# A hybrid decoder step on one core: where the attention's loads and stores stand in the DMA queue

## The chip, the cores and the metric

The kernel runs on one core of a Trainium2 chip. The metric is device time of the whole program in microseconds; the time before is the median of three runs. A profile of one further execution gives the trace that all rows below come from. Engines are PE (matrix multiplication, PEld its weight loads), DVE, ACT, POOL, and SP, which here does nothing but issue DMAs, one after another, in the order of its program. An SP instruction that waits for a buffer holds everything behind it.

## The reference

One inference step of a decoder with one recurrent layer (RG-LRU) and one attention layer with forget gates (FoX), for a prompt of 2048 new tokens and for 8 sequences of 8 new tokens with 4096 cached tokens each. Keys, values and log forget values are made once after the recurrent layer. The attention and what follows it, cut to what matters:

```python
def fox_block(q, k, v, cq, ck, q_pos, k_pos):
    s = jnp.einsum('bqhd,bkhd->bhqk', q, k).astype(jnp.float32) * (HEAD_DIM ** -0.5)
    s = s + jnp.swapaxes(cq, 1, 2)[:, :, :, None] - jnp.swapaxes(ck, 1, 2)[:, :, None, :]
    mask = k_pos[None, :] <= q_pos[:, None]
    s = jnp.where(mask[None, None], s, -jnp.inf)
    p = jax.nn.softmax(s, axis=-1)
    return jnp.einsum('bhqk,bkhd->bqhd', p.astype(v.dtype), v)
...
def fox_mixer(x, k, v, cq, ck, q_pos, k_pos, w_in, w_out):
    z = x @ w_in
    q, g = z[..., :D_ATTN].reshape(B, T, N_HEADS, HEAD_DIM), z[..., D_ATTN:]
    o = fox_attention(q, k, v, cq, ck, q_pos, k_pos).reshape(B, T, D_ATTN)
    return (o * jax.nn.silu(g)) @ w_out
...
past_k = cache_k[page_table].reshape(Bs, past_len, N_HEADS, HEAD_DIM)
past_v = cache_v[page_table].reshape(Bs, past_len, N_HEADS, HEAD_DIM)
```

There are 16 heads of 64, and a page of the cache holds 128 tokens. For the prompt, keys are the new tokens themselves; for the 8 sequences they are 32 cached pages each and the 8 new tokens. Everything is float32.

## The kernel before

The program runs in phases: the recurrent layer, the projections to keys, values, queries and gates (phase_b), the attention of the prompt, and the output projection. The decode, which is the attention of the 8 sequences over their cached pages, has no phase of its own: it is a generator (decode, line 1038) that a Side object (line 1011) advances a little after every step of the projections or of the prompt's attention. So two streams of work are interleaved on all engines.

**The order of instructions.** The Python code traces instructions one after another. A scheduler of the framework then puts the instructions of each engine into their final order, by a modelled timeline, with the order of tracing as priority: an instruction whose inputs and buffer are modelled as free earlier can be placed ahead of one that was traced before it. On the chip the order is fixed, and each instruction waits for semaphores where it stands. Two helpers add order by hand: issue_after(ins) places what a block traces on the engine of ins behind ins, without any wait for ins to finish; behind("V" or "T", ins) does the same against the newest instruction that the dictionary `place` holds for DVE or PE.

**The decode.** A turn is one sequence and half of its heads; there are 16, two of them in an early decode and 14 in the one that runs beside the later projections and the attention (called with ahead=True, lines 1812 to 1820). A turn reads 8 groups of 4 key pages and 8 groups of 4 value pages. pages (line 1075) issues one group, here called a page for short: four DMAs of 256 KB (line 1088) into one of 4 buffers named raw. DVE transposes a key page into ktr (line 1173), PE multiplies it with the queries into dS (line 1141); PE multiplies a value page with the numerators sx into dO (line 1251). Between keys and values stands softmax (line 1181): maxima, exponentials, sums, then a DVE transpose into sy, which takes a raw buffer for it, four stores of sy to DRAM (pd, line 1231), and a load back in another layout (sx, line 1232). period (line 1287) interleaves value pages 5 to 7 of the previous turn and key pages of the next one with steps of softmax: after each of the first seven pages two steps of it are taken, in the order v5, k0, v6, k1, v7, k2, k3, and what is left of it before v0.

**The prompt's attention** (line 1323) goes through 16 heads; a head has four units, one for each chunk of 512 queries, in rising order in even heads (4, 8, 12 and 16 blocks of 128 keys) and falling in odd ones. One block of scores is one step of the loop at line 1551, a tick: 40 ticks a head, 640 in all. A tick has two matmuls of scores (lines 1557 and 1558: qa with ka, qbt with kbt), an exponential on ACT into p or, for the first block, acc (line 1566), and every four ticks the products with the values vvt into ops (line 1577), after which POOL adds p into acc. Row maxima for units ahead are made by advance (line 1512) through the matmuls sx of line 1420 and DVE reductions (lines 1422 and 1424).

The loads of attention, all on SP but the very first:

- load_low(u + 2) at the start of unit u loads qa, 256 KB, 4 buffers (line 1408);
- load_keys (lines 1388 and 1389) loads kbt of the next head at tick 0 of a head;
- load_head (lines 1395 and 1396) loads ka (1 MB, 2 buffers) and vvt (512 KB) of the next head at tick 3;
- load_unit (line 1402) loads qbt as advance needs it.

After every second head norm (line 1481) inverts the sums and for each of the four chunks fetches the gates sgt (line 1501, 2 buffers), multiplies them with the head pair's output on POOL and with the inverted sums on DVE, and stores the product to og_d (line 1497). A Later object (line 349) runs closures a given number of ticks on: fetches at 3, 5, 7 and 9 ticks, each gate 3 ticks after its fetch, its store with it. For the last head pair the chunks go one by one as they end. The output projection reads og_d.

Of the kernel before, what the change touches and what calls it, by code (L numbers as in the profile page):

```python
# [20 lines left out]
P = 128  # L21
# [6 lines left out]
H = 16  # L28
# [29 lines left out]
ADD = "G"  # L58
OG = 1
NQ = 6  # L60


class Turns:
# [23 lines left out]
def tile_hawk_fox(  # L87
# [8 lines left out]
    V, A, G, T, S = nc.vector, nc.scalar, nc.gpsimd, nc.tensor, nc.sync  # L96
# [12 lines left out]
    place = {}  # L109

    def behind(engine, ins):

        if engine in place:
            tc.add_manual_dep(ins, place[engine].name, ORDER)

    def together(mms, after=(), beside=False):

# [53 lines left out]
    og_d = [dt_(f"ogd{qc}", [D, 512]) for qc in range(SEQ // 512)]  # L171
# [866 lines left out]
    def decode(es, turns, nraw, nktr, ahead):  # L1038
# [36 lines left out]
        def pages(cache, b, hg, g):  # L1075

            with ExitStack() as order:

                if len(last) >= 3:
                    order.enter_context(tc.issue_after(last[-3]))  # L1080
                regs = nc.values_load_multi_w_load_instructions(
                    pt1[0:1, b * NPG + g * 4:b * NPG + g * 4 + 4], engines=[SP], min_val=0, max_val=NPOOL - 1,
                    skip_runtime_bounds_check_because="the table was held between the first page and the last")[1]
            raw = pool.tile([P, 4, 512], F32, name="raw", tag="raw", bufs=nraw)
            came = []
            for i in range(4):
                page = cache[ds(regs[i], 1), :, hg * 8:(hg + 1) * 8, :]
                d = S.dma_start(raw[:, i, :], page.rearrange("o k h d -> (o k) (h d)"))
                came.append(d)
            last.append(d.ins)  # L1090
            return raw, came

        def new_rows(rows, b, hg):
# [87 lines left out]
        def softmax(t):  # L1181

            dl = t.dl
            b, hg, gmx = t.b, t.hg, t.gmx
            if not ahead:
                t.raws = [pages(cache_v, b, hg, x) for x in range(2)]
            while dl.q:
                dl.tick()
                yield HOP

            V.tensor_reduce(mx[:, :8], gmx[:, :, :].rearrange("p g h -> p h g"), axis=AX.X, op=ALU.max)
            mp = bank("dm")
            T.transpose(mp[:, :P], mx[:, :], ident[:, :])
            m1 = pool.tile([8, DS], F32, name="dm1", tag="dm1")
            V.tensor_reduce(m1[:, :], mp[:8, :P].rearrange("h (a q) -> h q a", q=DS), axis=AX.X, op=ALU.max)
            V.tensor_scalar(mr[:8, :, :], m1[:, :].unsqueeze(1).to_broadcast([8, 16, DS]), -1.0, 0.0, op0=ALU.mult, op1=ALU.add)
            T.matmul(mp[:, P:P + 8], mr[:, :, :].rearrange("h a q -> h (a q)"), ident[:, :8], start=True, stop=True)
            nm = pool.tile([P, 8], F32, name="dnm", tag="dnm")
            V.tensor_copy(nm[:, :], mp[:, P:P + 8])
            if t.next and t.next[1] == 0:  # L1200
                fetch_q(t.next[0])
            yield 3 * HOP

            ss = pool.tile([P, 2, 8], F32, name="dss", tag="dss")
            tt(V, t.cn[:, :, :], t.cn[:, :, :], nm[:DS, :].unsqueeze(2).to_broadcast([DS, 8, DS]), ALU.add)
            A.activation(pn[:DS, :, :DS], t.cn[:, :, :], AF.Exp)
            V.tensor_reduce(ss[:DS, 1, :], pn[:DS, :, :DS], axis=AX.X, op=ALU.add)
            for j in range(4):
                for h in (2 * j, 2 * j + 1):
                    A.activation(t.sc[:, :, h, :], t.sc[:, :, h, :], AF.Exp, bias=nm[:, h:h + 1], accum_out=ss[:, 0, h:h + 1])  # L1210
                if t.next:
                    place_q(*t.next, j)
                yield HOP
            tt(V, ss[:DS, 0, :], ss[:DS, 0, :], ss[:DS, 1, :], ALU.add)
            dg = pool.tile([P, 8, DS], F32, name="ddg", tag="ddg")
            tt(V, dg[:, :, :], ss[:, 0, :].unsqueeze(2).to_broadcast([P, 8, DS]),
               qmask[:, :].unsqueeze(1).to_broadcast([P, 8, DS]), ALU.mult)
            sp = bank("dsum")
            T.matmul(sp[:, :64], ones[:, :], dg[:, :, :].rearrange("p h q -> p (h q)"), start=True, stop=True)
            rb = t.rb = pool.tile([P, 64], F32, name="drb", tag="drb", bufs=2)  # L1220
            V.reciprocal(rb[:, :], sp[:, :64])


            sy = spare()[:, :].rearrange("p (a x h q) -> p a x h q", a=4, x=8, h=8)
            for h in range(8):
                V.transpose(sy[:, :, :, h, :].rearrange("p a x q -> p x a q"), t.sc[:, :, h, :])

            sx = pool.tile([P, 4, 8, 8, DS], F32, name="sx", tag="sx")
            pd = pd_d[(b * 2 + hg) % 2]
            for i in range(4):  # L1230
                S.dma_start(pd[:, :, i].rearrange("a l f -> l a f"), sy[i * 32:(i + 1) * 32].rearrange("p a x h q -> p a (x h q)"))
            S.dma_start(sx[:, :, :, :, :].rearrange("p i x h q -> p (i x h q)"), pd.rearrange("a l i f -> (a l) (i f)"))
            pt = pool.tile([32, 8, 32], F32, name="dpt", tag="dpt")
            V.transpose(pt[:, :, :].rearrange("p h x -> p (h x)"), pn[:, :, :].rearrange("p h x -> p (h x)"))
            pc = t.pc = pcs[(b * 2 + hg) % 2]
            A.copy(pc[:32, :].rearrange("p (h q) -> p h q", h=8), pt[:, :, :DS])
            t.sx = sx
# [85 lines left out]
    def attention(es):  # L1323
# [67 lines left out]
        def load_head(h):  # L1391
            hr = slice(h * HD, (h + 1) * HD)
            ka = pool.tile([P, SEQ], F32R, name="ka", tag="ka", bufs=2)
            for lo, hi in halves(h):
                queue[0].dma_start(f(ka[:, lo:hi]), kd_d[h * HD:(h + 1) * HD, :, lo:hi].rearrange("d x t -> (d x) t"))
            queue[0].dma_start(vvs[h % 2][:, :, :], v_d[:, hr].rearrange("(k p) d -> p k d", p=P))
            heads[h] = ka
# [6 lines left out]
        def load_low(u):  # L1404
            if u < len(units):
                h, qc = units[u]
                qa = qas[u] = pool.tile([P, 512], F32R, name="qa", tag="qa", bufs=4)
                queue[0].dma_start(f(qa[:, :]), qd_d[h * HD:(h + 1) * HD, :, qc * 512:(qc + 1) * 512].rearrange("d x t -> (d x) t"))
# [72 lines left out]
        def norm(pr, sums, q0, n, oT):  # L1481

            ps_ = slice(q0 * 32, (q0 + n) * 32)
            V.reciprocal(sums[ps_, :], sums[ps_, :])
            rs = [pool.tile([P, 32], F32R, name=f"rs{x}", tag=f"rs{x}") for x in range(2)]
            V.tensor_copy(rs[0][ps_, :], sums[ps_, :])
            tt(V, rs[1][ps_, :], sums[ps_, :], f(rs[0][ps_, :]), ALU.subtract)
            for x in range(2):
                to = rr[x * 8:(x + 1) * 8, :] if n == 4 else rr[x * 8 + q0:x * 8 + q0 + 5:4, :]
                S.dma_start(f(to).rearrange("j (r c) -> j r c", r=16), f(rs[x][ps_, :]))  # L1490

            def gate(qc, sg):
                ps = ps3.tile([P, 512], F32, name="rp", tag="sx", bufs=3)
                T.matmul(ps[:, :], sel[:, qc, :], rr[:, :], start=True, stop=True)
                tt(G, sg[:, :], sg[:, :], oT[qc - q0][:, :], ALU.mult)
                tt(V, sg[:, :], sg[:, :], ps[:, :], ALU.mult)
                S.dma_start(og_d[qc][pr * P:(pr + 1) * P, :], sg[:, :])

            def fetch(qc):
                sg = pool.tile([P, 512], F32, name="sgt", tag="sgt", bufs=2)  # L1500
                S.dma_start(sg[:, :], sg_d[pr * P:(pr + 1) * P, qc * 512:(qc + 1) * 512])
                later.after(3, lambda: gate(qc, sg))

            for qc in range(q0, q0 + n):
                later.after((3 if n == 4 else 0) + 2 * (qc - q0), lambda qc=qc: fetch(qc))

        tasks = [(u, j, ck) for u, (h, qc) in enumerate(units) for j in range(4) for ck in range(qc + 1)]
        nks = [(qc + 1) * 4 for _, qc in units]
# [32 lines left out]
        def scores_bank():  # L1541
# [4 lines left out]
                    return psum["dec"].tile([P, 512], F32, name="st", tag="do"[wide[0] // 2 % 2], bufs=1)  # L1546
            return ps3.tile([P, 512], F32, name="st", tag="st", bufs=2)

        for u, (h, qc) in enumerate(units):
            load_low(u + 2)  # L1550
            for k in range(nks[u]):
                ka, kb = heads[h], kbs[h % 2]
                qa, qb = qas[u], qbs[u % NQ]
                lo = max(0, k - qc * 4) * P
# [40 lines left out]
                later.tick()  # L1595
                if k + sum(nks[u - u % 4:u]) == 0 and h + 1 < H:
                    load_keys(h + 1)
                if k + sum(nks[u - u % 4:u]) == 3 and h + 1 < H:
                    load_head(h + 1)
                yield 4.1 * (512 - lo) * 0.42 + (done[0] - before) * 213  # L1600

    lent, dec_done = {}, []
# [264 lines left out]
```

## Time and profile before

| | |
|---|---|
| median of 3 runs | 3042.69 us (3035.71 to 3044.54) |
| the profiled execution, its own time | 3040.0 us |
| its span, first to last instruction | 3037.7 us |
| busy in the span | PE 2807.0 us (92%), DVE 1794.9 (59%), ACT 1267.6 (42%), POOL 1080.6 (36%) |
| mean granted clock of PE | 0.968 |
| moved by DMA | 653.39 MB, 215 GB/s over the span |
| loads of pages | 512 of keys and 512 of values, 256 KB each |
| other DMAs that the change touches | qa 62, ka 15, vvt 15, sgt 32, og_d 32 (on SP), pd 64 over both decodes |

How to read it: the page of the profile gives busy times, the chain of work that ended last and the costliest groups. A row of the waits names who waited, for whom, the microseconds in total, the times and the longest. A row of the timeline has the start, the duration, the engine (SPq is SP's queue of issues), the line, what is written from what, how many instructions were merged, and in brackets the idle time before it with what ended it. The duration of a row of SPq is the issue itself, not the transfer; a row that merges four issues has the time from the first to the last. In the chain, a piece named DMA runs from the issue to the landing. PEclk is the granted clock, 1 being full.

### The profile page before, as it was taken

To read this page: it belongs to the slowest core of one execution; us is meant where nothing else is said; L and a number is where in the kernel's file an instruction comes from. 1 tells how busy PE (TensorE), PEld (TensorE's weight loads), DVE (VectorE), ACT (ScalarE), POOL (GpSimd) and SP (SyncE) were. 2 spreads that over 40 slices of the span, in tenths; PEclk is the share of its full clock that TensorE was granted. 3 is DMA by queue.
4 is the path that set the end of the run, shared out by engine and by line. 5 is a ranking of instruction groups with operands and counts; after the bars stand their busy time and mean duration, and the time that the engine had idled before them with its cause. 6 is when DMAs were issued, how large, how long until landed. Compare 5 with 4: busy or idle time off the path is not lost.

```text
span 3037.7 us, 60435 instructions
## 1 busy us (share of the span) xinstructions
PE 2807.0 (92%) x21614; PEld 2250.1 (74%) x21614; DVE 1794.9 (59%) x4012; ACT 1267.6 (42%) x2874; POOL 1080.6 (36%) x1199
## 2 busy tenths in 40 slices
PE   5998999999999989999999699999999998999998
PEld 5997789989999978888897455555555655555687
DVE  7876455425357765765655465656566666665344
ACT  4665442222346654433333244344444444355321
POOL 1653201000016532000001455656555665558422
PEclk9999999999999999999999799999999999999999
DMA  4224546788622265999999888798889897974343
GB/s 122 85 82 137 173 125 196 244 265 270 221 85 87 78 193 177 312 330 348 343 327 334 245 247 245 242 297 254 254 260 283 251 273 241 285 230 109 96 146 110
DMA packets 478526, 653.39 MB, mean 215 GB/s; under 512 B 91099, under 2 KB 276444, under 8 KB 470949
## 3 DMA queue, kind: packets, MB, share of 16 engines
q1 hardware_dynamic: 474598, 643.87, 67.5%
q10 hardware_dynamic: 3340, 3.56, 0.4%
q8 instruction: 171, 2.80, 0.4%
q0 software_dynamic: 288, 2.10, 0.2%
q14 instruction: 129, 1.06, 0.1%
HBM read 513.82 MB, written 135.16 MB: 214 GB/s over the span
## 4 chain that ended last, share of the span: by engine, by line
PE 56%; DMA 13%; DVE 5%; ACT 4%; SPq 3%; issue 3%; POOL 1%; ACTq 0%; DVEq 0%; POOLq 0%
PE ops L1577 7%; PE st L1557 4%; PE dO L1251 4%; PE dS L1141 4%; PE sx L1420 4%; PE kv L378 3%; PE kv L379 3%; PE kv L380 3%; DMA raw<-in_cache_v_dram 3%; PE y L379 3%; PE y L378 3%; PE y L380 3%; PE st L1558 3%; PE qg L378 2%; PE qg L380 2%
## 5 line engine op out<-in xcount | busy, mean ns | idle before, releaser
L107 POOL TENSOR_TENSOR acc<-acc,p 128x512 f32<-128x512 f32 (+3 forms) x576 | 639.4, 1111 | 427.0 <-PE ops L1577 243.6
L1566 ACT ACTIVATE p<-st 128x512 f32<-128x512 f32 (+3 forms) x576 | 290.1, 525 | 424.2 <-PE st L1558 204.5
L1173 DVE STREAM_TRANSPOSE ktr<-raw 128x1024 f32<-128x1024 f32 x256 | 308.0, 1226 | 106.2 <-DMA raw<-in_cache_k_dram 94.0
L1422 DVE TENSOR_REDUCE mxs<-sx 128x1 f32<-128x512 f32 x384 | 254.4, 682 | 189.3 <-PE sx L1420 187.9
L378 PE MATMUL kv<-wh,xh 128*128 128x256 f32 (+3 forms) x1088 | 310.1, 289 | 7.3 <-ACT wh L422 7.3
L379 PE MATMUL kv<-wl,xh 128*128 128x256 f32 (+3 forms) x1088 | 307.7, 286 | 2.9 <-DVE wl L423 2.7
L380 PE MATMUL kv<-wh,xl 128*128 128x256 f32 (+3 forms) x1088 | 307.9, 285 | 0.0
L1557 PE MATMUL st<-qa,ka 128*128 128x512 f32 (+3 forms) x640 | 272.9, 427 | 19.5 <-ACT p L1566 16.7
L1577 PE MATMUL ops<-p,vvt 128*64 128x256 f32 (+1 forms) x2176 | 263.9, 369 | 4.4 <-ACT p L1566 4.0
L1420 PE MATMUL sx<-kbt,qbt 96*128 96x512 f32 (+3 forms) x640 | 233.3, 422 | 35.2 <-DMA qbt<-qd 19.0
L422 ACT ACTIVATE wh<-wst,gv 128x256 fp32r<-128x256 f32 (+1 forms) x384 | 164.6, 499 | 187.1 <-DMA wst<-in_w_kv_dram 68.0
L1558 PE MATMUL st<-qbt,kbt 128*128 128x512 f32 (+3 forms) x640 | 237.6, 373 | 0.0
L423 DVE SCALAR_TENSOR_TENSOR wl<-wst,gv,wh 128x256 fp32r<-128x256 f32 (+1 forms) x384 | 171.0, 494 | 109.9 <-ACT wh L422 107.9
L378 PE MATMUL qg<-xh,wh 128*128 128x384 f32 (+2 forms) x640 | 228.5, 358 | 0.0
L380 PE MATMUL qg<-xh,wl 128*128 128x384 f32 (+2 forms) x640 | 227.0, 355 | 1.2 <-DVE wl L423 1.2
L1577 PEld LDWEIGHTS ops<-p,vvt 128*64 128x64 f32 x2176 | 161.9, 141 | 88.5 <-issue 18.8
L379 PE MATMUL qg<-xl,wh 128*128 128x512 f32 (+2 forms) x640 | 227.2, 356 | 0.0
L1557 PEld LDWEIGHTS st<-qa,ka 128*128 128x128 f32 x640 | 124.6, 195 | 118.2 <-issue 55.0
L378 PEld LDWEIGHTS kv<-wh,xh 128*128 128x128 f32 (+1 forms) x1088 | 202.9, 188 | 12.5 <-ACT wh L422 9.0
L1106 POOL TENSOR_TENSOR qw<-qb,amask 128x128 f32<-128x128 f32 x64 | 29.8, 470 | 503.1 <-PE dS L1141 268.4
L379 PEld LDWEIGHTS kv<-wl,xh 128*128 128x128 f32 (+1 forms) x1088 | 202.8, 187 | 6.7 <-DVE wl L423 3.7
L380 PEld LDWEIGHTS kv<-wh,xl 128*128 128x128 f32 (+1 forms) x1088 | 204.0, 188 | 3.1 <-issue 3.1
(297 smaller groups left out, 6332.3 us busy)
## 6 DMA issues: line engine op xcount, KB each, us to landing
raw<-in_cache_k_dram SPq DMA_DIRECT2D x512, 256.0 KB
raw<-in_cache_v_dram SPq DMA_DIRECT2D x512, 256.0 KB
wst<-in_w_kv_dram SPq DMA_DIRECT2D x48, 512.0 KB
wst<-in_b_w_in_dram SPq DMA_DIRECT2D x48, 512.0 KB
xt<-in_x_prompt_dram SPq DMA_DIRECT2D x32, 512.0 KB
wst<-in_a_w_in_dram SPq DMA_DIRECT2D x64, 256.0 KB
out_dram<-kf SPq DMA_DIRECT2D x128, 128.0 KB
sc<-cd SPq DMA_DIRECT2D x16, 1024.0 KB
```

Source lines behind the costliest of these rows:

```text
L107: eng.tensor_tensor(out, a, b, op=op)
L378: T.matmul(ps, lh(k), rh(k), start=(k == 0), stop=False)
L379: T.matmul(ps, lh(k), rl(k), start=False, stop=False)
L380: T.matmul(ps, ll(k), rh(k), start=False, stop=(k == nk - 1))
L423: V.scalar_tensor_tensor(wl[:, k, :], st[:, k, :], gk, f(wh[:, k, :]), op0=ALU.mult, op1=ALU.subtract)
L1173: behind("V", V.transpose(t.kts[pp][:, n], raw[:, :, pp * 256:(pp + 1) * 256]).ins)
L1420: T.matmul(ps[:, :w], qb[0:96, j * P:(j + 1) * P], kb[0:96, ck * 512:ck * 512 + w], start=True, stop=True)
L1422: place["V"] = V.reduce_max(mx[:, j, ck:ck + 1], ps[:, :w], axis=AX.X).ins
L1557: place["T"] = T.matmul(ps[:, lo:], ka[:, ks], qa[:, lo:], start=True, stop=False).ins
L1558: T.matmul(ps[:, lo:], kb[:, ks], qb[:, lo:], start=False, stop=(k < qc * 4))
L1566: pair.append((k, lo, p, A.activation(p[:, lo:], ps[:, lo:], AF.Exp)))
L1577: return T.matmul(ops[r * HD:(r + 1) * HD, a0 * P:], vvs[h % 2][:, k, :], p[:, :].rearrange("p (a r c) -> p a r c", a=2, r=2)[:, a0:, r, : ...
```

## The change

The newest page's last DMA is kept in `place["S"]` by the later decode, and a helper paged() opens a block whose DMAs on SP are placed behind it. Under it stand now the loads of qa, of ka and vvt, of the gates, the stores of the gated product, and the numerators' stores pd. Besides, most of these are traced later:

- qa of unit v: at the later of the start of unit v - 2 and 14 ticks (AFT) after the start of unit v - 3, but at the latest 3 ticks before its own start; units 2 and 3 at the start of unit v - 2 as before;
- ka and vvt of the next head: at tick 16 instead of 3;
- the store of the gated product: 14 ticks after its multiplications (not for the last head pair);
- the gate fetches of chunks 2 and 3: at 24 and 26 ticks instead of 7 and 9; chunks 0 and 1 at 3 and 5 as before;
- pd: after four more steps of softmax, which in the order of period is after k2 instead of after k1.

The load of sx, those of kbt and qbt, and all computation stay as they are.

```diff
+AFT = 14
...
+    def paged():
+
+        return tc.issue_after(place["S"]) if "S" in place else ExitStack()
...
             last.append(d.ins)
+            if ahead:
+                place["S"] = d.ins
             return raw, came
...
+            if ahead:
+                for _ in range(4):
+                    yield 0
             sx = pool.tile([P, 4, 8, 8, DS], F32, name="sx", tag="sx")
             pd = pd_d[(b * 2 + hg) % 2]
-            for i in range(4):
-                S.dma_start(pd[:, :, i].rearrange("a l f -> l a f"), sy[i * 32:(i + 1) * 32].rearrange("p a x h q -> p a (x h q)"))
+            with paged() if ahead else ExitStack():
+                for i in range(4):
+                    S.dma_start(pd[:, :, i].rearrange("a l f -> l a f"), sy[i * 32:(i + 1) * 32].rearrange("p a x h q -> p a (x h q)"))
...
-                S.dma_start(og_d[qc][pr * P:(pr + 1) * P, :], sg[:, :])
+
+                def store():
+                    with paged():
+                        S.dma_start(og_d[qc][pr * P:(pr + 1) * P, :], sg[:, :])
+
+                if n == 4:
+                    later.after(AFT, store)
+                else:
+                    store()
...
-                S.dma_start(sg[:, :], sg_d[pr * P:(pr + 1) * P, qc * 512:(qc + 1) * 512])
+                with paged():
+                    S.dma_start(sg[:, :], sg_d[pr * P:(pr + 1) * P, qc * 512:(qc + 1) * 512])
...
-                later.after((3 if n == 4 else 0) + 2 * (qc - q0), lambda qc=qc: fetch(qc))
+                later.after((3 + 2 * (qc % 2) + (AFT + 7) * (qc // 2) if n == 4 else 2 * (qc - q0)), lambda qc=qc: fetch(qc))
...
+        lows = [2]
+
+        def loads():
+            while lows[0] < len(units):
+                v = lows[0]
+                if tick < (start[v - 2] if v < 4 else min(max(start[v - 2], start[v - 3] + AFT), start[v] - 3)):
+                    break
+                with paged():
+                    load_low(v)
+                lows[0] += 1
+            h, k = divmod(tick, 40)
+            if k == 16 and h + 1 < H:
+                with paged():
+                    load_head(h + 1)
+
         for u, (h, qc) in enumerate(units):
-            load_low(u + 2)
             for k in range(nks[u]):
+                loads()
...
-                if k + sum(nks[u - u % 4:u]) == 3 and h + 1 < H:
-                    load_head(h + 1)
```

## The prediction

> **What bounds the kernel now.** I read the page first, then busy time by stage, then the waits of PE and of the SP queue within the stage that the change touches, and last the timelines around the longest waits.
>
> ```profile
> span 3037.7 us, 60435 instructions
> ...
> PE 56%; DMA 13%; DVE 5%; ACT 4%; SPq 3%; issue 3%; POOL 1%; ACTq 0%; DVEq 0%; POOLq 0%
> ```
>
> The chain of waits goes mostly through PE and next through DMA. The busy times of two stretches show where the two meet (columns: stretch, length, busy time and instructions of each engine, granted clock, DMA share, GB/s):
>
> ```profile
> core 0: us, PE busy (x) PEld busy (x) DVE busy (x) ACT busy (x) POOL busy (x), PEclk, DMA share, GB/s
> ...
> 1540.00:1710.00 170.00, 141.89 (x1306) 116.59 (x1304) 84.07 (x169) 45.23 (x119) 17.89 (x29) 0.88 0.97 309
> 1710.00:2720.00 1010.00, 925.94 (x8436) 590.94 (x8432) 633.45 (x1346) 435.66 (x1087) 585.36 (x563) 0.95 0.86 260
> ```
>
> From 1710 to 2720 us attention runs with the decode beside it, and nearly everything that the change moves stands there. PE is the bound, but not fully: 1010 - 925.94 = 84.1 us idle, and a clock of 0.95, which is 0.05 x 1010 = 50.5 us of clock not granted. What PE waits for there:
>
> ```profile
> PE dO L1251 <- DMA raw<-in_cache_v_dram: 30.2, 14, 6.0
> ...
> PE dS L1141 <- DVE ktr L1173: 4.9, 4, 3.4
> ```
>
> The largest cause is a late value page (30.2 us in 14 waits); a late key page costs another 4.9 us, through the DVE transposes. Together 35.1 us. Nothing waits for qa, ka, vvt or sgt in this stretch, so those transfers are early and the pages are late. Why pages are late stands in the waits of the SP queue, which issues all of them in order:
>
> ```profile
> SPq L1088 <- PE dO L1251: 34.8, 16, 4.1
> SPq L1408 <- PE st L1560: 29.5, 10, 11.5
> SPq L1088 <- DVE ktr L1173: 22.9, 13, 5.4
> SPq L1497 <- DVE sgt L107: 20.9, 11, 6.6
> SPq L1395 <- PE st L1560: 20.6, 6, 7.9
> ...
> SPq L1501 <- DMA ogd<-sgt: 7.8, 9, 3.5
> ```
>
> Pages (L1088) wait 34.8 + 22.9 = 57.7 us for their own buffers. But qa (L1408), ka (L1395), the gated store (L1497) and the gate load (L1501) hold the queue for 29.5 + 20.6 + 20.9 + 7.8 = 78.8 us while their buffers are still in use, and whatever page stands behind them waits too. The longest PE waits:
>
> ```profile
> 2009.76 1.07 PE L1251 MATMUL dO<-raw,sx 128*32 128x256 f32 x16 [3.67 <-DMA raw<-in_cache_v_dram]
> 2178.18 1.94 PE L1251 MATMUL dO<-raw,sx 128*32 128x256 f32 x16 [4.08 <-DMA raw<-in_cache_v_dram]
> 2219.48 1.93 PE L1251 MATMUL dO<-raw,sx 128*32 128x256 f32 x16 [2.33 <-DMA raw<-in_cache_v_dram]
> 2518.53 1.94 PE L1251 MATMUL dO<-raw,sx 128*32 128x256 f32 x16 [5.97 <-DMA raw<-in_cache_v_dram]
> 2526.93 1.07 PE L1251 MATMUL dO<-raw,sx 128*32 128x256 f32 x16
> ```
>
> The same sixteen matmuls take 1.07 us at full clock and 1.93 after most of these gaps: a late page costs its gap and then some time at half rate. And the queue before the 5.97 us gap:
>
> ```profile
> 2501.17 0.34 SPq L1395 DMA_DIRECT2D ka<-kd  x1
> ...
> 2503.38 0.38 SPq L1396 DMA_DIRECT2D vvt<-vd  x1
> 2503.80 7.86 SPq L1402 DMA_DIRECT2D qbt<-qd  x1
> 2512.82 1.95 SPq L1088 DMA_DIRECT2D raw<-in_cache_v_dram  x4
> ```
>
> A head's ka and vvt go out together, the issue behind vvt is held 7.86 us, and the page leaves only at 2512.82. PE wants it from 2518.53 - 5.97 = 2512.56.
>
> **The change, part by part.** No arithmetic and no byte is added or taken away. Four kinds of DMA get another place in SP's order.
>
> *Loads of qa, ka and vvt.* They are traced later (qa by up to 14 ticks, ka and vvt at tick 16 of a head instead of 3) and pinned behind the newest page. This should take away the SP waits at L1408 and L1395, and it parts ka and vvt from kbt, which stays at tick 0. *The gated store* is traced 14 ticks after its multiplications, so the DVE result that it waits for is there; the gate loads for chunks 2 and 3 come 21 ticks after the first two, past those stores. This takes the 20.9 and the 7.8 us.
>
> The gain is bounded from above by all page waits: 35.1 us idle, and their part of the clock lost. 35.1 / 84.1 of the stage's idle time is 0.42; 0.42 x 50.5 = 21; as half-rate stretches partly overlap the gaps themselves I count half, 10.5. Ceiling 45.6 us. From below it is nothing, if the pages' own buffers set them. Between the two I take the share of the queue's holding time that the change removes, 78.8 / (78.8 + 57.7) = 0.58, so 0.58 x 45.6 = 26 us.
>
> The Trainium skill ("TensorE: Matmul & The Clock Gate", What's actually happening) says that the clock falls to half after an idle window of about 3.4 us. The rows above bear it out only in part: 2.33 us was enough at 2219.48, and 3.67 us did nothing at 2009.76. By that rule alone the three gaps over 3.4 us that stand here would lose some 1.7 us each, an estimate of 5 us instead of the 10.5, and the sum would end 3 us higher.
>
> *What may come late instead.* A load of qa now is traced as little as three ticks before its unit (units 1 and 2 of the seven even heads after the first, 14 loads). One tick is a block of scores, of which there are 640:
>
> ```profile
> L1566 ACT ACTIVATE acc<-st x64: 570/597/601, 1706.9 to 2833.0; 128x512 f32<-128x512 f32 x64
> ```
>
> (2833.0 - 1706.9) / 636 = 1.77 us, so three ticks are 5.3 us. Two landings of qa stand in the chain of waits:
>
> ```profile
> 1694.62 10.79 DMA qa<-qd
> ...
> 2742.92 4.84 DMA qa<-qd
> ```
>
> Behind a page's issue (1.95 us above) a load needs 1.95 + 7.8 (the mean of the two) = 9.8 us. It has 5.3 us plus the lead of the page in SP's order over its use in PE's, and even for the late page above that was 2518.53 - 2512.82 = 5.7 us: 11.0 us, enough on average and 1.95 + 10.79 - 11.0 = 1.7 us short at worst. Bounds: 0, and 14 x (1.95 + 10.79 - 5.3) = 104 us if the page had no lead at all. I take a quarter of the worst shortfall at each, 14 x 0.43 = 6 us. If PE waits on qa, the scores, ACT's exponentials and POOL's additions are late behind it. ka and vvt have 24 ticks (42 us), and the later gate loads are hidden by the second half of their head pair, 29 of 80 ticks.
>
> *The numerators' stores.* In most turns pd already stands right behind the third key page:
>
> ```profile
> 1860.88 1.89 SPq L1088 DMA_DIRECT2D raw<-in_cache_k_dram  x4
> 1862.87 2.10 SPq L1231 DMA_DIRECT2D pd<-sy  x3
> ```
>
> so the pin changes nothing there. In one turn it split a value page, ahead of the 4.08 us gap:
>
> ```profile
> 2164.25 0.36 SPq L1088 DMA_DIRECT2D raw<-in_cache_v_dram  x1
> ...
> 2165.47 3.16 SPq L1231 DMA_DIRECT2D pd<-sy  x4
> 2168.84 2.73 SPq L1088 DMA_DIRECT2D raw<-in_cache_v_dram  x3
> ```
>
> That gain, at most 3.2 us, is inside the 26. Cover against the later store: sx was issued at 1872.12, and its first product came at 1893.72:
>
> ```profile
> 1872.12 10.93 DMA sx<-pd
> ```
> ```profile
> 1893.72 1.07 PE L1251 MATMUL dO<-raw,sx 128*32 128x256 f32 x16
> ```
>
> It landed 10.7 us before its use; a delay beyond that would be PE idle in each of 14 turns. I cost it at nothing. The stretch after 2720 has no pages, so its pins are idle.
>
> **Sum.** -26 + 6 = -20 us. The profiled execution took 3040.0 us by its own time (the span and 2.3 us around it); the median of the runs is 2.7 above it. 3040.0 - 20 + 2.7 = 3023 us.
>
> **The rivals.**
>
> *All page waits go* (0.13): the queue's holding also caused the pages' own buffer waits, since a late product frees its buffer late, and qa costs nothing. 3042.7 - 45.6 = 2997. Against it: 57.7 us of the pages' waits are for their own buffers, and the change takes no time out of what fills and frees those.
>
> *The stall moves* (0.20). The 7.86 us behind vvt stays, and now a page is always near behind it, where here a qbt took it.
>
> ```profile
> L1088 SPq FUSED_REGOPS  x636: 37/46/57, 1699.5 to 2707.0; - x159
> ```
>
> 159 pages in 1007.5 us are one per 6.3 us; a page held 7.86 us is 1.5 us late, 15 heads make 23 us, and -20 + 23 = +3: 3046, no change to speak of. DMA's share of 0.86 speaks for it, and against it that 0.97 and 309 GB/s were reached in the stretch before. The Trainium skill ("DMA: Bandwidth & Descriptors", Issuing engines are not separate DMA queues) has all transfers on the same 16 engines, whoever issues them; by that an order of issue adds no bandwidth, and the trace's unchanged work would go this way.
>
> *Slower: qa late* (0.22). Place: the first matmul of units 1 and 2 of an even head. With no page lead each of the 14 loads is 9.8 - 5.3 = 4.5 us short, 63 us; against the 26 gained that is +37, 3080. It decides from 14 x (4.5 - lead) = 26 on, a lead under 2.6 us. For it: pages wait for buffers too, and what is pinned behind a waiting page waits with it. Against: the 5.7 us of the late page.
>
> The forecast itself has 0.45, with a range of its own of 3007 to 3034.
>
> **How the numbers follow.** No change means within 0.3%, 9 us, about what a measurement of this kernel can tell. Faster: 0.45 + 0.13 = 0.58; same: 0.20; slower: 0.22. The range reaches from below the second case, 2990, to 3060: it holds the forecast, the first two rivals, and a qa that is late at about two thirds of its loads (+42 - 26 = +16); what is left out is the rest of the slower case.
>
> **What would show it.** Right: SP's waits at L1408, L1395, L1497 and L1501 fall from 78.8 to below 20 us; PE's wait for value pages from 30.2 to about 13; the clock from 1710 to 2720 rises above 0.95. The step on late loads is wrong if PE waits for qa by more than some 6 us in total, the numerators' step if PE waits for sx at all. The forecast is wrong if the page waits stay near 30 us with the held loads gone: then the buffers set the pages; or if a new wait of PE on a pinned load is as large as what was removed.

## The result and the profile after

The changed kernel takes 3035.56 us (median of 18 runs, 3019.93 to 3041.59) against 3043.97 us of the kernel before on the same chips: a ratio of 0.9965, 95% interval [0.9953, 0.9977]. It is faster, by 8.4 us where 20 were forecast. Its profiled execution took 3036.55 us, with a span of 3034.8.

The same stretches as before the change, from the busy times by stage of the changed kernel:

```profile
1540.00:1710.00 170.00, 145.06 (x1381) 124.33 (x1379) 83.83 (x164) 48.81 (x126) 17.67 (x29) 0.93 0.99 316
1710.00:2720.00 1010.00, 925.70 (x8485) 589.78 (x8486) 641.76 (x1373) 438.97 (x1096) 586.25 (x563) 0.96 0.86 264
```

Fixed stretches hide the difference, since the stream of work has shifted in them. Cut instead at the first and the last exponential that writes acc, which is where attention begins and ends. First the kernel before, then the changed one (length, then PE busy; PEclk is third from the right):

```profile
0.00:1706.90 1706.90, 1578.88 (x11684) 1439.12 (x11688) 1021.63 (x2290) 724.21 (x1556) 346.67 (x513) 0.98 0.64 207
1706.90:2833.00 1126.10, 1032.86 (x9077) 656.88 (x9073) 688.69 (x1456) 500.97 (x1225) 682.03 (x644) 0.95 0.81 244
```
```profile
0.00:1722.50 1722.50, 1586.66 (x11711) 1444.21 (x11711) 1017.52 (x2282) 723.76 (x1556) 344.57 (x513) 0.97 0.64 205
1722.50:2829.40 1106.90, 1020.45 (x9046) 649.54 (x9046) 690.72 (x1465) 501.77 (x1226) 682.57 (x644) 0.97 0.81 249
```

Attention takes 1106.9 us instead of 1126.1: 19.2 less. PE's idle time (length less busy) falls from 93.2 to 86.5, by 6.8; its busy time falls from 1032.86 to 1020.45, by 12.4, at a granted clock of 0.97 instead of 0.95. The two cuts don't hold quite the same work (9077 and 9046 matmuls in the rows): in the changed kernel 28 products of a value page stand ahead of the first exponential that stand behind it before. From the 11461st matmul, up to which PE's order is the same in all versions, to the last score there are 9318 matmuls in both, and the difference is again 19.2 us: 1183.2 and 1164.0, idle 7.6 less and busy 11.7 less. But attention begins 15.6 us later, 1722.5 against 1706.9, and what follows it has the same length, 205.4 against 204.7. So 19.2 - 15.6 - 0.7 = 2.9 us is the difference of these two spans.

What PE waits for from 1710 to 2720 us in the changed kernel (total, times, longest):

```profile
PE dO L1262 <- DMA raw<-in_cache_v_dram: 23.5, 17, 2.8
...
PE dS L1148 <- DVE cn L108: 6.2, 1, 6.2
...
PE st L1592 <- DMA qa<-qd: 4.7, 2, 4.4
...
PE dO L1262 <- DMA sx<-pd: 2.3, 1, 2.3
...
PE dS L1148 <- DVE ktr L1180: 1.6, 3, 1.2
```

Late value pages cost 23.5 us in place of 30.2. They are more, but each is short: the longest is 2.8 where it was 6.0. And the SP queue's waits in the same stretch:

```profile
SPq L1093 <- PE dO L1262: 38.5, 18, 10.2
SPq L1399 <- PE st L1595: 25.8, 7, 10.2
SPq L1093 <- DVE ktr L1180: 23.8, 12, 6.9
SPq L1093 <- DVE mxs L1435: 16.4, 8, 7.1
...
SPq L1093 <- DVE mxs L1433: 11.4, 5, 5.9
...
SPq L1413 <- PE st L1595: 11.2, 5, 5.9
...
SPq L1511 <- DVE sgt L108: 9.2, 4, 8.4
...
SPq L1521 <- DMA ogd<-sgt: 6.9, 5, 3.7
...
SPq L1419 <- PE st L1595: 5.4, 1, 5.4
```

The lines have moved: pages are L1093, ka L1406, qa L1419, the gated store L1511, the gate load L1521. The four waits of the forecast fall from 78.8 us to 5.4 + 0 + 9.2 + 6.9 = 21.5. The queue isn't freer for that: a page now stands at its front and waits itself (two rows on mxs that were not among the large ones before). All rows of the pages' issues together rise from some 120 us to some 203. And kbt, which the change left where it was, waits 25.8 us for the buffer that the scores still read.

### The profile page after: what moved, and what is told of

The parts are those of the page before. It is cut to its first block, busy times and chain, and to the rows that moved or that the text cites. A ratio compares the mean times of both kernels' runs of the same rounds, so it can differ in the third digit from the quotient of the medians.

```text
span 3034.8 us, 60405 instructions
## 1 busy us (share of the span) xinstructions
PE 2803.1 (92%) x21614; PEld 2247.9 (74%) x21614; DVE 1793.3 (59%) x4012; ACT 1267.8 (42%) x2874; POOL 1079.0 (36%) x1199
## 2 busy tenths in 40 slices
DMA packets 478527, 653.40 MB, mean 215 GB/s; under 512 B 91099, under 2 KB 276444, under 8 KB 470949
## 4 chain that ended last, share of the span: by engine, by line
PE 46%; DMA 20%; DVE 6%; ACT 4%; SPq 4%; issue 3%; POOL 2%; DVEq 0%; ACTq 0%; POOLq 0%
PE ops L1612 5%; DMA raw<-in_cache_k_dram 5%; DMA raw<-in_cache_v_dram 4%; PE st L1592 3%; PE dO L1262 3%; PE y L383 3%; PE y L385 3%; PE y L384 3%; PE sx L1431 3%; PE kv L385 3%; PE kv L383 3%; PE kv L384 3%; PE dS L1148 2%; PE st L1593 2%; SPq L1093 2%
```

## The experiments

Each version is the changed kernel with parts of it undone. In the table "held" is the sum of the forecast's four SP waits, each with the one cause that the forecast named, and "V waits" PE's wait for value pages, both from 1710 to 2720 us; idle and busy are PE's between the first and the last exponential into acc, as in the rows above. The kernel before on the same chips had medians of 3044.64 (e1 to e4), 3043.19 (e5 to e8) and 3044.95 (e9 to e12).

| version | median us | ratio to before | attention | idle | busy | held | V waits |
|---|---|---|---|---|---|---|---|
| before | | 1 | 1126.1 | 93.2 | 1032.9 | 78.8 | 30.2 |
| the change | 3035.56 | 0.9965 [0.9953, 0.9977] | 1106.9 | 86.5 | 1020.5 | 21.5 | 23.5 |
| e1 without the pd edit | 3027.79 | 0.9938 [0.9922, 0.9955] | 1107.2 | 90.0 | 1017.3 | 32.5 | 26.3 |
| e2 pd edit alone | 3041.27 | 0.9989 [0.9974, 1.0004] | 1125.9 | 97.2 | 1028.8 | 78.8 | 27.1 |
| e3 all late, no pins | 3039.42 | 0.9980 [0.9967, 0.9992] | 1116.5 | 94.9 | 1021.6 | 96.4 | 30.7 |
| e4 all pinned, not late | 3055.06 | 1.0036 [1.0022, 1.0050] | 1136.6 | 100.3 | 1036.3 | 56.3 | 27.6 |
| e5 the change again | 3036.44 | 0.9974 [0.9954, 0.9994] | 1108.5 | 92.3 | 1016.2 | 20.0 | 23.6 |
| e6 qa alone | 3035.20 | 0.9975 [0.9954, 0.9996] | 1116.8 | 86.5 | 1030.3 | 69.1 | 22.9 |
| e7 head at tick 16 alone | 3068.66 | 1.0065 [1.0039, 1.0091] | 1150.0 | 104.4 | 1045.6 | 79.8 | 24.0 |
| e8 gates alone | 3024.83 | 0.9932 [0.9905, 0.9959] | 1098.7 | 78.1 | 1020.7 | 71.4 | 23.7 |
| e9 qa and gates | 3026.38 | 0.9941 [0.9924, 0.9958] | 1103.4 | 85.6 | 1017.8 | 62.2 | 22.1 |
| e10 head at tick 28 alone | 3024.85 | 0.9935 [0.9915, 0.9954] | 1105.7 | 83.6 | 1022.1 | 73.1 | 14.6 |
| e11 gates late, no pins | 3032.49 | 0.9965 [0.9948, 0.9982] | 1110.1 | 80.5 | 1029.6 | 95.8 | 29.3 |
| e12 gates alone, again | 3024.99 | 0.9944 [0.9926, 0.9963] | 1100.3 | 79.8 | 1020.5 | 73.2 | 26.9 |

**The numerators' edit.** First the change without it, then it alone.

```diff
-                for _ in range(4):
+                for _ in range(0):
                     yield 0
...
-            with paged() if ahead else ExitStack():
+            with ExitStack():
                 for i in range(4):
```

> The change without its edit of the numerators' stores (no four steps, no pin of pd); the attention's loads and stores as changed. Theory A (the attention's part is worth about 20 us, and the pd edit gives some 10 of them back in the projections before 1720 us): ratio to before 0.991 to 0.995, better than the change's 0.9965; first exponential of attention back near 1707 us, attention still some 1107 us long. Theory B (the pd edit is neutral, the later start of attention in the changed profile is that execution's own): ratio 0.9955 to 0.9975. Theory C (the gain is the pd edit's): ratio 0.999 to 1.001.

> The kernel before with the pd edit alone (four more steps and the pin). Theory A: slower, ratio 1.002 to 1.004, attention begins later than before. Theory B: ratio 0.999 to 1.001. Theory C: 0.996 to 0.998.

Alone the edit does nothing that can be told (an interval with 1 in it, attention 1125.9 against 1126.1). Without it the rest is some 8 us faster, 3027.79 against 3035.56 and 3036.44, and the intervals of the ratios barely overlap. In attention there is no difference, 1107.2 against 1106.9 and 1108.5; in the profiles it stands ahead of attention, which starts at 1712.3 in e1 and at 1722.5 and 1722.3 with the edit.

**Lateness and pins apart.** e3 keeps the later tracing and replaces every `with paged():` of the change by `with ExitStack():`. e4 keeps the pins and traces everything where it was:

```diff
-                if tick < (start[v - 2] if v < 4 else min(max(start[v - 2], start[v - 3] + AFT), start[v] - 3)):
+                if tick < start[v - 2]:
...
-            if k == 16 and h + 1 < H:
...
+                if k + sum(nks[u - u % 4:u]) == 3 and h + 1 < H:
```

> All as in the change but without any pin: the later tracing alone. Theory A says that a load traced later still goes out as soon as its buffer is modelled as free, so most of the held time of the queue is back (over 50 of the 78.8 us) and the ratio is 0.998 to 1.002. Theory D (later tracing is what counts, since it lowers the loads' priority against pages): ratio 0.996 or below, held time as low as in the change.

> The pins alone, all tracing times as before. Theory A: a load pinned behind the newest page but traced when its buffer is still in use waits there with pages behind it, so about half of the gain, ratio 0.996 to 1.000, with SP's waits at qa and ka over 30 us. Theory D: no gain, ratio 1.000 or above.

Neither half is the change. Late without pins gains about 10 us of attention; pinned without being late loses 10, though its four waits are well under those of before:

```profile
SPq L1511 <- DVE sgt L108: 18.8, 7, 7.2
SPq L1419 <- PE st L1591: 18.1, 3, 11.1
SPq L1406 <- PE st L1591: 15.1, 4, 6.7
...
SPq L1521 <- DMA ogd<-sgt: 4.3, 6, 2.2
```

That is 56.3 us held, against 78.8, and the kernel is slower, 1.0036 [1.0022, 1.0050]. In e3 96.4 us are held, and it is faster. This is the first sign that held time is the wrong measure.

**One kind of transfer at a time.** With the change run again beside them: only qa, only ka and vvt, only the gates' loads and stores, each late and pinned, all else as before.

> The change as it is, once more, on the chip of the three kernels below, to set beside the kernel without the pd edit (0.9938). Theory A (the pd edit costs some 8 us beside the other parts): ratio 0.9955 to 0.9975 again, and attention in the trace some 1107 us long as it was without the edit. Theory B (pd neutral, chips and executions differ): ratio 0.993 to 0.995.

> Of the change only the loads of qa are later and pinned. Held time of the queue at qa was 29.5 of 78.8 us. Theory A (each part brings its share): -10 us + 6 us for late loads, ratio 0.997 to 1.000, attention 1118 to 1124 us long. Theory E (the queue is one; a part alone only moves the holding to the next load): ratio 0.999 to 1.002, held time at ka and the gates higher than before. Theory F (the loads of ka and vvt are the cause): 0.999 to 1.001.

> Only the loads of ka and vvt are later (tick 16) and pinned. Theory A: 20.6 of 78.8 us held, -7 us, ratio 0.997 to 0.9985. Theory E: 0.999 to 1.002. Theory F: most of the gain, ratio 0.993 to 0.996.

> Only the gates' loads and the gated stores are later and pinned. Theory A: 28.7 of 78.8 us held, -9 us, ratio 0.996 to 0.998. Theories E and F: 0.999 to 1.002.

The gates alone give more than the whole change, 0.9932 against 0.9974; ka and vvt alone cost 0.65%. Where in attention the time goes is seen by heads. Cut at the first exponential into acc of each head, and summed over the six even heads 2 to 12 and the seven odd ones 1 to 13:

| | before | change | e5 | e6 qa | e7 head 16 | e8 gates | e9 | e10 head 28 | e11 | e12 gates | e4 |
|---|---|---|---|---|---|---|---|---|---|---|---|
| even heads, us | 466 | 454 | 461 | 452 | 500 | 442 | 445 | 465 | 450 | 445 | 489 |
| odd heads, us | 487 | 488 | 483 | 494 | 478 | 488 | 488 | 475 | 493 | 485 | 477 |

In the kernel before, the gated stores of a head pair go in the even head that follows it, and most of the gate loads too, and there the gates' part gains 17 to 25 us in all four versions that have it without the head's (e8, e9, e11, e12), with the odd heads as before within 6. The loss of e7 stands in the even heads too: 34 us. The heads don't hold the same decode work in every version, though: in the even ones PE starts 3917 matmuls before, 4096 in e7, 3871 in e8 and 3797 in e6, so part of each difference is work that moved between even and odd heads. One thing that goes wrong in e7 shows in SP's queue, in head 2, and in the matmuls after it:

```profile
1908.98 0.33 SPq L1511 DMA_DIRECT2D ogd<-sgt  x1
1913.57 0.33 SPq L1521 DMA_DIRECT2D sgt<-sgd  x1
1914.01 0.37 SPq L1511 DMA_DIRECT2D ogd<-sgt  x1
1919.35 0.32 SPq L1521 DMA_DIRECT2D sgt<-sgd  x1
1920.36 1.90 SPq L1093 DMA_DIRECT2D raw<-in_cache_k_dram  x4
1922.81 1.92 SPq L1093 DMA_DIRECT2D raw<-in_cache_v_dram  x4
```
```profile
1930.99 1.93 PE L1262 MATMUL dO<-raw,sx 128*32 128x256 f32 x16 [5.62 <-DMA raw<-in_cache_v_dram]
...
1940.94 1.93 PE L1262 MATMUL dO<-raw,sx 128*32 128x256 f32 x16 [3.28 <-DMA raw<-in_cache_v_dram]
```

A store of the gated product goes out, and right behind it stands the gate load into the same buffer, which waits 4 to 5 us until the store has landed; then the next pair does the same, and for some 12 us no page leaves. PE has two long gaps behind that. In the row of the waits:

```profile
SPq L1521 <- DMA ogd<-sgt: 26.6, 12, 5.6
```

against 7.8 us in 9 waits before. With the gates late and pinned (e8) the same place of head 2 looks so:

```profile
1908.43 0.42 SPq L1511 DMA_DIRECT2D ogd<-sgt  x1
1908.90 0.43 SPq L1521 DMA_DIRECT2D sgt<-sgd  x1
1910.52 1.92 SPq L1093 DMA_DIRECT2D raw<-in_cache_k_dram  x4
1913.00 0.33 SPq L1521 DMA_DIRECT2D sgt<-sgd  x1
1913.95 2.49 SPq L1093 DMA_DIRECT2D raw<-in_cache_v_dram  x4
1917.06 1.89 SPq L1093 DMA_DIRECT2D raw<-in_cache_k_dram  x4
1920.95 1.92 SPq L1093 DMA_DIRECT2D raw<-in_cache_v_dram  x4
```

No load waits for the store ahead of it, and pages leave every 3 to 4 us.

This isn't the bulk of e7's loss, though. Over its even heads PE waits 18.0 us for value pages, against 17.9 before. Its waits for the inverted sums rise from 4.1 to 10.9 us, and its busy time from 421.0 to 443.1, with 179 more matmuls and a granted clock of 0.923 instead of 0.962. What lowers the clock there isn't shown.

The gates' part doesn't have the pd edit, and that may be all of its lead in time: the change without that edit (e1) is level with it, 0.9938. In attention alone the gates stay ahead, 1098.7 against 1107.2.

**Parts together, the head elsewhere, gates without pins, and the best one again.** e10 is e7 with one number changed:

```diff
-            if k == 16 and h + 1 < H:
+            if k == 28 and h + 1 < H:
```

> Keeps the later, pinned qa and the later, pinned gate loads and stores; the heads' ka and vvt and the numerators' stores stand as before. First to last exponential of attention: 1126 us before, 1107 and 1108 in the whole change, 1099 with the gate part alone, 1117 with qa alone. If the parts add, 1126 - 27 - 9 = 1090 and a ratio near 0.990. If one queue has one holding to lose and the gate part has taken it already, 1097 to 1101 and 0.993, the same as the gate part alone. If the head's part is needed in the whole change, 1107 or more and 0.997.

> Only ka and vvt are moved, as in the slower run that had them alone at tick 16 (attention 1150 us, ratio 1.0065), but to tick 28. Collision theory: at tick 16 the 1.5 MB of a head fell on the norm of the pair of heads (its gate loads and stores at ticks 3 to 12 of an even head, held there); at tick 28 that is over, so attention is back at 1121 to 1130 us and PE's waits for the inverted sums at some 4 us, ratio 0.999 to 1.001. Rival: ka and vvt pinned behind a page cost wherever they stand, since the issue behind vvt is held for 5 to 8 us and a page follows; then attention stays at 1140 to 1150 and the ratio at 1.004 to 1.007.

> Only the gated stores 14 ticks after their multiplications and the loads for chunks 2 and 3 at 24 and 26 ticks; no pin. If the lateness is what brings the gate part's gain (it takes the wait for the product out of SP's queue), attention takes 1097 to 1104 us, as with the pins, and the ratio is 0.993 to 0.995. If the place behind the newest page is what counts, it takes 1116 to 1126 us and the ratio is 0.998 to 1.000, with SP still held at the gated store by over 15 us.

> The gate part alone once more, as the measure of how far one such number holds: attention took 1098.7 us and the ratio was 0.9932. If the gate part alone is better than the whole change, attention is again below 1103 and the ratio below 0.9955, the lower end of the whole change's two intervals being 0.9953 and 0.9954. If the difference to the whole change was chance of one profile, attention is at 1105 to 1110 and the ratio at 0.996 to 0.998.

The gates alone are better than the whole change on another chip too: 3024.99, 0.9944, attention 1100.3. qa adds nothing to them (0.9941). Without pins they gain about half (0.9965), with 14.8 and 16.2 us of the stores' and loads' waits left; the intervals of e11 and e12 overlap, so the pin's share isn't settled to better than that. Those two waits are 31.0 us together, more than the 28.7 before, and attention is still 16.0 us shorter. So the gates' gain isn't just that these holds go away, and what it is made of isn't shown.

e10 is faster than was thought: 0.9935, the rival of a cost wherever the head stands is out, and so is the price of 0.999 to 1.001 that the collision theory gave. Its mechanism isn't borne out either: ka leaves 24 us into head 4 in e7 and 33 us in e10, while the gates' stores stand at 52 to 65 and 46 to 63 us, so the later head is the one that is nearer to them. In e10 the gain is in the odd heads (475 against 487) and outside the table (head 14 takes 51.4 us instead of 59.0), and its page waits are the smallest of all, although qa's load is held longer than before (48.8 us against 29.5):

```profile
SPq L1419 <- PE st L1595: 48.8, 16, 7.2
...
SPq L1521 <- DMA ogd<-sgt: 12.3, 8, 4.4
...
SPq L1511 <- DVE sgt L108: 12.0, 5, 6.4
```
```profile
PE dO L1262 <- DMA raw<-in_cache_v_dram: 14.6, 13, 3.6
```

Twelve ticks of one pair of loads thus move the ratio from 1.0065 to 0.9935, some 40 us. The framework's scheduler orders the queue anew around it: between e7 and e10 about 150 of SP's 2461 issues that are not ka or vvt stand in another place. So a version tells the worth of an order, not of a part.

## Why the prediction was right, and where it wasn't

**What bounds the stage** was right: PE, with the late pages and the clock as what can be won, and the queue's order as the way to it. Of attention's 19.2 us some 10 are page waits and some 12 PE's busy time at a better clock, while its other waits grew by about 3.

**The sum over attention** was right, 20 us forecast and 19.2 and 17.6 (1126.1 - 1108.5) measured, but not its terms, so that the total came out is luck. The forecast took 0.58 of 35.1 us of page waits, 20.4, and 0.58 of 10.5 for the clock, 6.1. Measured, page waits fell from 35.1 to 23.5 + 1.6 = 25.1, by 10.0, half of what was counted; PE's busy time, where the clock shows, fell by 12.4 (11.7 with the same matmuls), twice as much.

**The measure of the gain failed.** "The share of the queue's holding time that the change removes" was to give the gain. The change removes 57 of the 78.8 us, nearly as forecast (21.5 left, "below 20"). But the table's versions refute the rule: 71.4 to 73.2 us still held gain 20 to 27 us of attention (e8, e10, e12), 56.3 lose 10 (e4), 79.8 lose 24 (e7), 95.8 and 96.4 gain 16 and 10 (e11, e3). It isn't the choice of rows: with every cause of a wait counted, the four lines wait 100.5 us before, 41.8 in the change, 123.7 in e8 and 104.9 in e7. PE's waits for value pages don't tell it either, 23.7 in e8 and 24.0 in e7. It would fit that a hold costs only where a page that PE needs soon stands behind it, but no run tests that by itself.

**The late qa** was priced too high at 6 us. PE waits 4.7 us for qa in the change, but 4.4 of it is the very first score of attention:

```profile
1715.38 0.76 PE L1592 MATMUL st<-qa,ka 128*128 128x512 f32 x1 [4.39 <-DMA qa<-qd]
```

It reads the qa of unit 0, whose load the change leaves as it was, and e7 (4.47) and e10 (4.62) have the same wait with all qa as before. For loads that were traced later PE waits 0.35 us in the change, 2.4 in e5 and at most 5.0 (e9), each time at one unit. The rival that qa would be short at 14 loads is refuted, although the shortest time from issue to use in the change is 7.1 us (2594.96 to 2602.05).

**All page waits go** didn't happen: 25.1 of 35.1 us remain.

**The stall that moves** did move: the issue behind vvt is still held, and now it often is a page's, as here in the change:

```profile
2317.99 0.50 SPq L1407 DMA_DIRECT2D vvt<-vd  x1
2319.35 6.56 SPq L1093 DMA_DIRECT2D raw<-in_cache_k_dram  x4
```

But at 1.5 us a head it was to cost 23 us, and attention got 19.2 us shorter, with no wait for a value page over 2.8 us. Behind the hold shown here, PE's next two groups of value products (2322.60 and 2335.20) wait for no page; that the four buffers take it up is a reading, which no run tests. The rival's price was wrong, not its place.

**The numerators' edit at nothing** holds for the time of the edit alone (e2). By the forecast's own sign, PE waiting for sx at all, the step is wrong by little: the change has one such wait of 2.3 us, before it there was none. Beside the other parts it goes with about 8 us (e1), which no step of the forecast has.

**What the forecast left out** is the time ahead of attention: "3040.0 - 20 + 2.7" takes it as unchanged. In the two profiles of the change attention starts at 1722.5 and 1722.3, in the twelve others, the one of before among them with 1706.9, at 1705.5 to 1716.7. That may be what lies between the 19 us of attention and the 8.4 of the medians. Part of it is spread: by the 8000th matmul, up to which all versions run the same instructions in the same order, they are at 1275.5 to 1288.0 us, the profile of before at 1277.9, the change at 1284.6 and 1288.0. From there to the 11461st it is 383.9 and 378.7 us in the change, 378.6 with the pd edit alone, 374.4 before, and 375.7 to 379.4 in the other versions. So the profile of before was an early one, and of the two of the change one is slow there and one is not. That the edit costs time there is not shown, and why the medians show 8 stays open. Nothing was run that tells it apart.

**The clock.** The forecast read that a gap of 3.67 us did nothing. The first sixteen matmuls behind it did run at full rate, but from 2010.70 to 2014.10 the granted clock is 0.50, so it fell 0.9 us after they began. And the stage had five gaps over 3.4 us, not three: the forecast's list leaves out one of 3.61 and one of 3.62. The Trainium skill ("TensorE: Matmul & The Clock Gate", What's actually happening) has the clock fall after about 3.4 us of idle. The change has two gaps of PE above that in attention, 6.2 and 3.7 us, yet at 0.97 the clock that is not granted is 0.03 x 1106.9 = 33 us. As before the change, gaps over the bound explain a small part of it: in the trace's record of the clock it falls 20 times in attention before and is at half for 99.0 us, 16 times and 71.7 us in the change, 15 times and 68.3 us in e8, which has no gap over 3.4 us there, and 20 times and 129.7 us in e7. Half of the difference to before is 15 us both ways, by this estimate some 15 of the 27 us that e8 gains and of the 24 that e7 loses. Shorter page gaps and a better clock came together here, but not in e6, whose longest page gap is 2.8 us and whose PE is busy 1030.3 us; what sets the clock isn't settled.

## What to carry to other kernels

The sum of the waits in a queue of issues is no price: here versions with more of it than the change gained more. Before pricing such a wait, take the next transfers one by one and ask when their users need them. A load that reuses the buffer of a store just issued waits for that store, 4 to 5 us each in e7, and the pages stand behind it; moving the gates alone was here better for attention than moving everything, though that these waits were the reason isn't shown. And when a scheduler orders the queue anew, run each part alone: one part beat the whole change by 11.6 us (3024.83 against 3036.44 on the same chip), and without its smallest edit, which alone did nothing that could be told, the change came level with that part (e1).

## What the runs showed of the hardware

The issue behind the 512 KB of vvt, 256 bytes a row, takes 4 to 9 us in 176 of the 210 cases of these fourteen traces and under 4 in 28, whatever it loads; the issue behind the 1 MB of ka takes 0.3 to 1.7 us. Moving instructions round it moves it only to another line. In these traces the granted clock is 1 or 0.5 and nothing between, and each stretch at half within attention lasts 3.4 us or a whole multiple of it. And the Trainium skill ("DMA: Bandwidth & Descriptors", Issuing engines are not separate DMA queues) has all transfers on the same 16 engines, whoever issues them. By that an order of issue would add no bandwidth, and the trace agrees roughly: 653.40 MB and 264 GB/s in the stage where it was 653.39 and 260. Still, orders of the same transfers lie some 40 us apart (e7 and e10).
